# Gate and up with a 512-wide product over both halves of the activations, and weight conversions 1024 wide, in a three-block network on one Trainium2 core

## The chip, the cores and the metric

One core of one Trainium2 chip runs the whole program. The metric is the device time of one launch in microseconds (us). Its engines are TensorE (PE; its weight loads are listed as PEld), VectorE (DVE), ScalarE (ACT), GpSimd (POOL) and SyncE (SP), which issues most DMAs.

## What is computed

The reference sends 256 tokens of width 1024 through two layers of a first block (feed forward, a mixer of retention and gated delta rule, attention to a memory, feed forward) and one second block (state space part, attention, feed forward). All is in float32. The part that the change touches is the feed forward, which occurs five times:

```python
def swiglu(u, w_gate, w_up, w_down):
    return (jax.nn.silu(u @ w_gate) * (u @ w_up)) @ w_down
```

Here `u` is [256, 1024], `w_gate` and `w_up` are [1024, 2816] and `w_down` is [2816, 1024].

## The kernel before

**Products in two parts.** TensorE multiplies in the type float32r, which keeps fewer digits than float32. So each operand is split into a high part, rounded to float32r, and a low part, the remainder, and a product is made of three: high by high, high by low, low by high. `mm3` (L169 to L171) issues these three matmuls. Activations are split where they are transposed (`to_xT`): the high part goes into a tile `xh`, the low part into a tile `xl`, each [128, 8, 256], which is 8 slices of 128 channels by 256 tokens.

**Weights.** `unit` (L133 to L150) loads 1024 columns of weights (512 KB) into one of four `raw` buffers by DMAs of SP's queue (L142). ACT rounds them into `hi` (L147) and DVE subtracts to give `lo` (L148), each in two instructions 512 wide, half after half. The `raw` buffer is free again when both have read it, and only then can SP's next load into it start. The unit lands in one of two pools of weight units, which run well ahead of PE.

**One feed forward (`ffn`).** The 2816 hidden channels go by in 11 groups `j` of 256. Groups 0 and 1 are made with tokens on partitions (`by_tokens`), groups 2 to 10 with channels on partitions: `by_channels(i, j)` makes tile i = 0 or 1 of 128 channels. With 9 groups, 2 tiles and 5 feed forwards there are 90 such tiles. One tile takes, for each of 8 slices k and for a = 0 (gate) and 1 (up), three matmuls of 256 columns: 48 matmuls into one PSUM bank, gate in its columns 0 to 255, up in 256 to 511. DVE then multiplies the bank by the tokens' factors (L400), ACT takes the tanh of the gate (L401), DVE makes the rest of silu and the product with up (L402, L403), and the result is split again into `hh` (ACT, L174) and `hl` (DVE, L176). L174 and L176 are lines of the helper `split`, which splits activations too.

**Order of the work.** `DN(t, j)` multiplies token tile t of group j by the down weights: 12 matmuls of 512 columns, of which the first 6 read tile i = 0 and the last 6 tile i = 1 of `hh` and `hl`. In the middle of a feed forward PE does, group after group,

```python
by_channels(0, j); DN(0, j - 1); by_channels(1, j); DN(1, j - 1)
```

so that tile i = 1 of group j has `DN(1, j - 1)`, the next group's tile i = 0, and half of `DN(0, j)` to be ready in. For j = 2 `DN(1, 0)` stands where `DN(0, 1)` would. The down weights of a group are asked for in `DN`, two units each (one for each i). In the two feed forwards named ffn1 a hook puts a part of the mixer's preparation behind each group. At the end come `DN(0, 8)` to `DN(0, 10)`, then `DN(1, 7)` to `DN(1, 10)`.

Each engine's instructions are put into a fixed order when the program is built, by a scheduler that weighs what each waits for; on the chip each engine takes its own list in that order. So where a weight conversion stands ahead of a tanh in ACT's list, the tanh waits for that conversion, and with it for the conversion's DMA. PSUM has 8 banks, 4 of which hold the sums of the down products in most of a feed forward.

Of the kernel before, what the change touches and what calls it, by code (L numbers as in the profile page):

```python
# [11 lines left out]
F32R = mybir.dt.float32r  # L12
# [10 lines left out]
# columns of the constant table  # L23
C_ID, C_TF, C_SUM, C_ONE = 0, 128, 256, 304
# the ones that only the first block reads
C_TB, C_Z0, C_DN, C_DP, C_HALF, C_END = 304, 432, 560, 944, 1328, 1332
# the ones that only the set-up reads
# [41 lines left out]

class Net:  # L70
    def __init__(self, ctx, tc, a):
# [25 lines left out]
        # instructions that the conversions of weights are queued behind  # L97
        self.fence = []

    def first_block(self, ctx):  # L100
        """what only the first block needs"""
# [17 lines left out]
    def more_weights(self):  # L119
        """a second pool of weight units, kept until no_more_weights()"""  # L120
        if self.w2 is None:
            self.w2_stack = ExitStack()
            self.w2 = self.w2_stack.enter_context(self.tc.tile_pool(name="w2", bufs=8, side="right", reuse_waits="tile"))
        return self.w2
# [9 lines left out]
    def unit(self, loads, n=1024, pool=None, into=None):  # L134
# [8 lines left out]
        with ExitStack() as es:  # L143
            for ins in self.fence:
                es.enter_context(self.tc.issue_after(ins))
            for c in (slice(0, n // 2), slice(n // 2, n)):
# [4 lines left out]
    def prime(self):  # L151
        """the first weights of the next stage, before what its activations wait for"""
# [4 lines left out]
    def unit_rows(self, w, k0, nk, c0, nc_, pool=None):  # L157
        """rows k0*128.. (nk tiles of 128) by columns c0..c0+nc_ of w, as [128, nk, nc_]"""
        hi, lo = self.rows_unit(w, k0, nk, c0, nc_, pool)
# [3 lines left out]
    def rows_unit(self, w, k0, nk, c0, nc_, pool=None, into=None):  # L163
        src = w[k0 * P:(k0 + nk) * P, c0:c0 + nc_].rearrange("(k p) c -> p k c", p=P)
        return self.unit([(lambda r: r[:, :nk * nc_].rearrange("p (k c) -> p k c", k=nk), src)], nk * nc_, pool, into)
# [18 lines left out]
    def rsqrt_half(self, vh, w, eng=None):  # L184
        """v ** -0.5 by Newton steps, given vh = v / 2 > 0 as [128, w]; the sign alternates, so it starts negative"""
# [13 lines left out]
    def half_squares(self, srcs, n):  # L199
        """sums of squares along rows over 2 n, one column for each source"""  # L200
# [16 lines left out]
    def bcast(self, pool, src, w, tag, eng=None):  # L217
        """a row of w values from memory, on all partitions"""
# [10 lines left out]
    def normed(self, src, g, r):  # L229
        """src * r * g, [128, 1024]"""  # L230
# [8 lines left out]
    def new_xT(self):  # L239
        return (self.xp.tile([P, 8, 256], F32R, tag="xh", name="xh"),  # L240
                self.xp.tile([P, 8, 256], F32R, tag="xl", name="xl"))

    def to_xT(self, src, xT, t, k0=0, nk=8, scale=1.0):
        """transposes [128 tokens, nk*128] into xT[:, k0.., t*128..], in two parts that add up exactly"""
# [8 lines left out]
    def set_pre(self, t, g, defer):  # L253
        """the normed activations of the next part: elementwise now, transposes when the part asks. With defer
        the tokens' factors 1 / rms are left to that part, as self.factor"""
# [23 lines left out]
    def run_late(self):  # L279
        """the end of the stage before that the second tokens still miss"""  # L280
# [23 lines left out]
    def gate_up(self, wg, wu, j, q, pool=None):  # L304
# [4 lines left out]
        return self.unit(loads, pool=pool)  # L309

    def ffn(self, wg, wu, wd, gpost_src, post, gpre_src, defer, hook=None, final=None):
        nc = self.nc
        with ExitStack() as es:
# [14 lines left out]
            def wpool(kind, j):  # L328
                # the last units but those for gate and up leave the lasting pool to the next stage
# [5 lines left out]
            def load_gu(j):  # L335
                return [[u.rearrange("p (k a f) -> p k a f", k=2, a=2) for u in self.gate_up(wg, wu, j, q, wpool("gu", j))] for q in range(4)]
# [10 lines left out]
            def by_tokens(t, j, between=None):  # L347
                """one token tile's hidden values, tokens on partitions"""
# [26 lines left out]
            def factor_rows():  # L375
                """half of 1 / rms of the tokens, along the columns of all partitions"""
# [7 lines left out]
            def by_channels(i, j):  # L384
                """one channel tile's hidden values, channels on partitions"""
                if j not in gu:
                    gu[j] = load_gu(j)
                b = self.bank()
                bb = b.rearrange("p (a c) -> p a c", a=2)
                xh, xl = xT  # L390
# [1474 lines left out]
```

## Time and profile before

| what | value |
|---|---|
| three timed runs | 1964.11, 1965.86, 1966.60 us (median 1965.86) |
| span of the profiled execution | 1964.9 us |
| granted clock of TensorE, mean | 0.998 of full speed |
| PE, busy | 1931.5 us (98%) |
| PE weight loads, busy | 1738.6 us (88%) |
| DVE, busy | 1400.5 us (71%) |
| ACT, busy | 1060.7 us (54%) |
| POOL, busy | 182.3 us (9%) |

The profiled execution is recorded by its span, from the first to the last instruction of the core; no other time of it is kept. Busy time of PE includes the time in which one matmul overlaps the next, so a PE that is 98% busy need not be at its peak: how far apart matmuls start says more. Times in a timeline count from the span's start.

### The profile page before, as it was taken

What the parts mean: (1) busy time and instruction counts of PE and PEld (TensorE: products, weight loads), DVE (VectorE), ACT (ScalarE), POOL (GpSimd) and SP (SyncE); (2) the same over time, 40 slices, a digit from 0 to 9 for tenths busy, and PEclk for the clock granted to TensorE, in tenths of its full rate; (3) what the DMA queues carried; (4) which work ended last, traced back from release to release, by engine and by line L of the source; (5) the groups of instructions that cost most, each with busy time, mean ns of one, the idle gap of its engine ahead of it and who ended that gap; (6) DMA issues with size and microseconds to landing.
All of it is one profiled execution on the core that took longest, in us unless ns stands there. A gap on an engine that the chain in (4) does not pass through costs nothing.

```text
span 1964.9 us, 34894 instructions
## 1 busy us (share of the span) xinstructions
PE 1931.5 (98%) x12971; PEld 1738.6 (88%) x12971; DVE 1400.5 (71%) x2981; ACT 1060.7 (54%) x2193; POOL 182.3 (9%) x407
## 2 busy tenths in 40 slices
PE   8999999999999999999999999999999999999998
PEld 6999988898899989999788988998999998888997
DVE  6776688575676666667885747766788988767665
ACT  6655566465555555546554645544555655546542
POOL 2000100020200120010100211002101101001000
PEclk9999999999999999999999999999999999999999
DMA  8666434265465557645433735655466647667651
GB/s 281 193 213 213 129 112 141 83 214 161 150 214 183 171 178 227 198 151 151 135 114 118 232 112 183 203 182 171 131 184 186 173 129 206 199 200 221 195 179 50
DMA packets 272889, 337.28 MB, mean 172 GB/s; under 512 B 19740, under 2 KB 223150, under 8 KB 272718
## 3 DMA queue, kind: packets, MB, share of 16 engines
q1 hardware_dynamic: 266980, 326.64, 53.8%
q10 hardware_dynamic: 5690, 8.25, 1.3%
q8 instruction: 102, 1.67, 0.3%
q14 instruction: 69, 0.57, 0.1%
q0 software_dynamic: 48, 0.16, 0.0%
HBM read 333.90 MB, written 1.08 MB: 170 GB/s over the span
## 4 chain that ended last, share of the span: by engine, by line
PE 82%; DVE 6%; DMA 3%; POOL 3%; issue 3%; ACT 2%; SPq 0%; ACTq 0%; DVEq 0%; POOLq 0%
PE bank L169 24%; PE bank L171 24%; PE bank L170 24%; DVE lo L148 3%; DMA raw<-in_ffn_up_dram 1%; PE bank L1145 1%; POOL t L191 1%; POOL vh L212 1%; PE bank L249 1%; POOL y L192 1%; DMA raw<-in_xattn_k_dram 1%; ACT hi L147 1%; PE bank L1002 1%; PE bank L1542 1%; ACT md L1033 1%
## 5 line engine op out<-in xcount | busy, mean ns | idle before, releaser
L148 DVE TENSOR_TENSOR lo<-raw,hi 128x512 fp32r<-128x512 f32 (+1 forms) x1190 | 765.3, 680 | 219.8 <-ACT hi L147 212.8
L147 ACT ACTIVATE hi<-raw 128x512 fp32r<-128x512 f32 (+1 forms) x1190 | 677.1, 615 | 425.9 <-PE bank L170 96.1
L169 PE MATMUL bank<-xh,hi 128*128 128x256 f32 x2080 | 591.1, 284 | 0.0
L171 PE MATMUL bank<-xh,lo 128*128 128x256 f32 x2080 | 586.8, 282 | 1.0 <-DVE lo L148 1.0
L170 PE MATMUL bank<-xl,hi 128*128 128x256 f32 x2080 | 586.0, 282 | 0.0
L169 PEld LDWEIGHTS bank<-xh,hi 128*128 128x128 f32 x2080 | 394.4, 190 | 3.9
L170 PEld LDWEIGHTS bank<-xl,hi 128*128 128x128 f32 x2080 | 394.3, 190 | 3.4
L171 PEld LDWEIGHTS bank<-xh,lo 128*128 128x128 f32 x2080 | 394.7, 190 | 1.4 <-DVE lo L148 1.4
L169 PE MATMUL bank<-hi,xh 128*128 128x512 f32 (+1 forms) x852 | 334.1, 393 | 5.7 <-ACT xh L174 5.4
L170 PE MATMUL bank<-lo,xh 128*128 128x512 f32 (+1 forms) x852 | 325.5, 382 | 4.4 <-DVE lo L148 4.4
L171 PE MATMUL bank<-hi,xl 128*128 128x512 f32 (+1 forms) x852 | 324.8, 382 | 3.2 <-DVE xl L176 3.2
L169 PEld LDWEIGHTS bank<-hi,xh 128*128 128x128 f32 x852 | 160.9, 189 | 35.0 <-ACT xh L174 7.8
L171 PEld LDWEIGHTS bank<-hi,xl 128*128 128x128 f32 x852 | 160.8, 189 | 33.6 <-DVE xl L176 7.0
L170 PEld LDWEIGHTS bank<-lo,xh 128*128 128x128 f32 x852 | 161.2, 189 | 32.1 <-DVE lo L148 7.3
L169 PE MATMUL bank<-hi,hh 128*128 128x512 f32 x440 | 175.6, 399 | 0.8 <-ACT hh L174 0.8
L171 PE MATMUL bank<-hi,hl 128*128 128x512 f32 x440 | 174.0, 395 | 0.0
L170 PE MATMUL bank<-lo,hh 128*128 128x512 f32 x440 | 173.8, 395 | 0.0
L212 POOL TENSOR_SCALAR vh<-ss 128x1 f32<-128x1 f32 x40 | 27.8, 695 | 1152.3 <-ACT junk L204 1016.0
L401 ACT ACTIVATE th<-s 128x256 f32<-128x256 f32 x90 | 37.3, 415 | 124.1 <-DVE s L400 122.6
L171 PEld LDWEIGHTS bank<-hi,hl 128*128 128x128 f32 x440 | 82.8, 188 | 20.2 <-DVE hl L176 0.2
L169 PEld LDWEIGHTS bank<-hi,hh 128*128 128x128 f32 x440 | 82.7, 188 | 17.4 <-ACT hh L174 1.3
L170 PEld LDWEIGHTS bank<-lo,hh 128*128 128x128 f32 x440 | 82.8, 188 | 16.4
(364 smaller groups left out, 2020.4 us busy)
## 6 DMA issues: line engine op xcount, KB each, us to landing
raw<-in_w_in_dram SPq DMA_DIRECT2D x112, 512.0 KB, 4.2
raw<-in_ffn_gate_dram SPq DMA_DIRECT2D x176, 256.0 KB, 3.9
raw<-in_ffn_up_dram SPq DMA_DIRECT2D x176, 256.0 KB, 4.3
raw<-in_ffn_down_dram SPq DMA_DIRECT2D x88, 512.0 KB, 4.5
raw<-in_w_in_dram SPq DMA_DIRECT2D x96, 192.0 KB, 2.8
raw<-in_w_ffn_gate_dram SPq DMA_DIRECT2D x44, 256.0 KB, 3.8
raw<-in_w_ffn_up_dram SPq DMA_DIRECT2D x44, 256.0 KB, 4.3
raw<-in_w_ffn_down_dram SPq DMA_DIRECT2D x22, 512.0 KB, 4.4
```

Source lines behind the costliest of these rows:

```text
L147: nc.scalar.activation(hi[:, c], raw[:, c], AF.Copy)
L148: nc.vector.tensor_tensor(lo[:, c], raw[:, c], hi[:, c].bitcast(F32), ALU.subtract)
L169: mm(out, lhsT=lh, rhs=rh, start=start, stop=False)
L170: mm(out, lhsT=lh, rhs=rl, start=False, stop=False)
L171: mm(out, lhsT=ll, rhs=rh, start=False, stop=stop)
L191: V.tensor_scalar(t, y, y, vh, ALU.mult, ALU.mult)
L192: V.tensor_scalar(y, t, -1.5, y, ALU.add, ALU.mult)
L212: V.tensor_scalar(vh, s[:, 0:1], s[:, 1:2], 0.5 * EPS, ALU.add, ALU.add)
L249: self.nc.tensor.transpose(b[:, i * P:(i + 1) * P], src[:, (q + i) * P:(q + i + 1) * P], self.ident)
L401: last["A"] = nc.scalar.activation(th, s[:, 0], AF.Tanh)
L1002: T.matmul(b[:, j * 256:(j + 1) * 256], lhsT=lhs[:, h, j * P:(j + 1) * P], rhs=rhs[:, h], start=True, stop=True)
L1033: A.activation(md[r, :, :, :, s], mn[r, :, :, c0:c0 + 16].rearrange("p n h a -> p a h n"), AF.Copy, scale=self.half[s][r])
```

## The change

It has two parts. First, the activations' two parts lie in one tile `xT` of [128, 2, 8, 256], behind a small class `Parts`, so that one matmul can stream the high and the low part of a slice, 512 columns, past the high weights. The products of the high and the low part then lie side by side in a bank, so that gate and up need a bank each. The low weights' matmul, 256 columns, adds to the first half. Afterwards ACT copies the second half to SBUF and DVE adds the first to it, once for gate and once for up; the multiplication by the factors then reads SBUF. Second, weights for gate and up from group 3 on, and down weights from group 2 on, are converted 1024 wide: one ACT and one DVE instruction for each unit in place of two each. The rest of the diff takes out comments.

```diff
+class Parts:
+    def __init__(self, tile_):
+        self.tile = tile_
+    def __getitem__(self, i):
+        if i > 1:
+            raise IndexError
+        return self.tile[:, i]
+    def both(self, k):
+        return self.tile[:, :, k]
...
-            for c in (slice(0, n // 2), slice(n // 2, n)):
+            for c in (slice(0, n),) if whole else (slice(0, n // 2), slice(n // 2, n)):
                 nc.scalar.activation(hi[:, c], raw[:, c], AF.Copy)
                 nc.vector.tensor_tensor(lo[:, c], raw[:, c], hi[:, c].bitcast(F32), ALU.subtract)
...
     def new_xT(self):
-        return (self.xp.tile([P, 8, 256], F32R, tag="xh", name="xh"),
-                self.xp.tile([P, 8, 256], F32R, tag="xl", name="xl"))
+        return Parts(self.xp.tile([P, 2, 8, 256], F32R, tag="xT", name="xT"))
...
-                return [[u.rearrange("p (k a f) -> p k a f", k=2, a=2) for u in self.gate_up(wg, wu, j, q, wpool("gu", j))] for q in range(4)]
+                return [[u.rearrange("p (k a f) -> p k a f", k=2, a=2) for u in self.gate_up(wg, wu, j, q, wpool("gu", j), j > 2)] for q in range(4)]
...
-                b = self.bank()
-                bb = b.rearrange("p (a c) -> p a c", a=2)
-                xh, xl = xT
+                mm = nc.tensor.matmul
+                b = [self.bank() for _ in range(2)]
                 c = slice(i * P, (i + 1) * P)
                 for k in range(8):
                     wh, wl = gu[j][k // 2]
                     for a in range(2):
-                        self.mm3(bb[:, a], wh[:, k % 2, a, c], wl[:, k % 2, a, c], xh[:, k], xl[:, k], k == 0 and a == 0, k == 7 and a == 1)
+                        mm(b[a].rearrange("p (a c) -> p a c", a=2), lhsT=wh[:, k % 2, a, c], rhs=xT.both(k), start=k == 0, stop=False)
+                        mm(b[a][:, 0:256], lhsT=wl[:, k % 2, a, c], rhs=xT[0][:, k], start=False, stop=k == 7)
...
-                nc.vector.tensor_tensor(s, bb, rows[0], ALU.mult)
+                for a in range(2):
+                    nc.scalar.copy(s[:, a], b[a][:, 256:512])
+                    nc.vector.tensor_tensor(s[:, a], b[a][:, 0:256], s[:, a], ALU.add)
+                nc.vector.tensor_tensor(s, s, rows[0], ALU.mult)
...
-                    dn[j] = [self.unit_rows(wd, 2 * j + q, 1, 0, D, wpool("dn", j)) for q in range(2)]
+                    dn[j] = [self.unit_rows(wd, 2 * j + q, 1, 0, D, wpool("dn", j), j > 1) for q in range(2)]
```

In the changed kernel the conversions are L161 and L162, the 512-wide matmul L408, the 256-wide one L409, the copy L415, the addition L416, the multiplication L417, the tanh L418, the two that follow L419 and L420, and the split L188 and L190.

The change alters what each engine's list holds and in which order. **PE**, at the start of tile i = 1 of group 2 in the fourth feed forward (ffn2 of the second layer). The names are the bank, the activations and the weights. Before:

```order
6627 L169 MATMUL bank_13862<-xh_13417,hi_13744 128x256
6628 L170 MATMUL bank_13862<-xl_13418,hi_13744 128x256
6629 L171 MATMUL bank_13862<-xh_13417,lo_13745 128x256
6630 L169 MATMUL bank_13862<-xh_13417,hi_13744 128x256
6631 L170 MATMUL bank_13862<-xl_13418,hi_13744 128x256
6632 L171 MATMUL bank_13862<-xh_13417,lo_13745 128x256
```

Of the change:

```order
5747 L408 MATMUL bank_12943<-xT_12510,hi_12836 128x512
5748 L409 MATMUL bank_12943<-xT_12510,lo_12837 128x256
5749 L408 MATMUL bank_12944<-xT_12510,hi_12836 128x512
5750 L409 MATMUL bank_12944<-xT_12510,lo_12837 128x256
5751 L408 MATMUL bank_12943<-xT_12510,hi_12836 128x512
5752 L409 MATMUL bank_12943<-xT_12510,lo_12837 128x256
```

Six matmuls of 256 columns into one bank became four, two of them of 512 columns, into two banks. The columns are the same in sum, and the order of PE's other work is kept.

**ACT**, around the tanh of the same tile. L147 (now L161) with a `hi` is a conversion of weights; the last two units ahead of `hh` in the second list, like the two on either side of the first list's `hh`, are down weights of group 3. Before:

```order
957 L147 ACTIVATE hi_13959<-raw_13958 128x512 x2
958 L147 ACTIVATE hi_14035<-raw_14034 128x512 x2
959 L147 ACTIVATE hi_14124<-raw_14123 128x512 x2
960 L147 ACTIVATE hi_14142<-raw_14141 128x512 x2
961 L401 ACTIVATE th_13912<-s_13911 128x256
962 L147 ACTIVATE hi_14151<-raw_14150 128x512 x2
963 L147 ACTIVATE hi_14219<-raw_14218 128x512 x2
964 L174 ACTIVATE hh_13839<-th_13912 128x256
965 L147 ACTIVATE hi_14227<-raw_14226 128x512 x2
```

Of the change:

```order
1050 L161 ACTIVATE hi_13160<-raw_13159 128x1024
1051 L415 COPY s_12977<-bank_12943 128x256
1052 L161 ACTIVATE hi_13174<-raw_13173 128x1024
1053 L415 COPY s_12977<-bank_12944 128x256
1054 L161 ACTIVATE hi_13181<-raw_13180 128x1024
1055 L161 ACTIVATE hi_13236<-raw_13235 128x1024
1056 L161 ACTIVATE hi_13242<-raw_13241 128x1024
1057 L418 ACTIVATE th_12978<-s_12977 128x256
1058 L188 ACTIVATE hh_12920<-th_12978 128x256
```

Before, the tanh stood ahead of both down conversions and `hh` between them; now the tanh and `hh` stand behind both.

**DVE**, at the same place. Before:

```order
1490 L400 TENSOR_TENSOR s_13911<-bank_13862,rows_13833 128x512
1491 L148 TENSOR_TENSOR lo_14143<-raw_14141,hi_14142 128x512 x2
1492 L402 SCALAR_TENSOR_TENSOR th_13912<-th_13912,s_13911 128x256
1493 L148 TENSOR_TENSOR lo_14152<-raw_14150,hi_14151 128x512
1494 L403 SCALAR_TENSOR_TENSOR th_13912<-th_13912,s_13911 128x256
1495 L148 TENSOR_TENSOR lo_14152<-raw_14150,hi_14151 128x512
1496 L148 TENSOR_TENSOR lo_14220<-raw_14218,hi_14219 128x512
1497 L176 TENSOR_TENSOR hl_13840<-th_13912,hh_13839 128x256
```

Of the change:

```order
1566 L416 TENSOR_TENSOR s_12977<-bank_12943,s_12977 128x256
1567 L162 TENSOR_TENSOR lo_13175<-raw_13173,hi_13174 128x1024
1568 L416 TENSOR_TENSOR s_12977<-bank_12944,s_12977 128x256
1569 L162 TENSOR_TENSOR lo_13182<-raw_13180,hi_13181 128x1024
1570 L417 TENSOR_TENSOR s_12977<-s_12977,rows_12910 128x512
1571 L162 TENSOR_TENSOR lo_13237<-raw_13235,hi_13236 128x1024
1572 L419 SCALAR_TENSOR_TENSOR th_12978<-th_12978,s_12977 128x256
1573 L162 TENSOR_TENSOR lo_13243<-raw_13241,hi_13242 128x1024
1574 L420 SCALAR_TENSOR_TENSOR th_12978<-th_12978,s_12977 128x256
1575 L190 TENSOR_TENSOR hl_12921<-th_12978,hh_12920 128x256
```

`lo_14220`, and in the second list `lo_13237` and `lo_13243`, belong to down units. The second of the two instructions behind the tanh (L403, now L420) stood ahead of both down units; now it stands behind both.

## Rows read from the trace of the kernel before

**Rows 1.** The page's first part: span, and busy time of each engine.

```profile
span 1964.9 us, 34894 instructions
PE 1931.5 (98%) x12971; PEld 1738.6 (88%) x12971; DVE 1400.5 (71%) x2981; ACT 1060.7 (54%) x2193; POOL 182.3 (9%) x407
```

**Rows 2.** The chain that ended last, by engine.

```profile
PE 82%; DVE 6%; DMA 3%; POOL 3%; issue 3%; ACT 2%; SPq 0%; ACTq 0%; DVEq 0%; POOLq 0%
```

**Rows 3.** All waits of PE; engine, line, releaser, us in all, times, longest.

```profile
PE bank L169 <- ACT hh L174: 0.8, 1, 0.8
```

**Rows 4.** Timeline of PE, group 2 of the fourth feed forward; start and duration in us.

```profile
1220.16 0.40 PE L169 MATMUL bank<-hi,hh 128*128 128x512 f32 x1
...
1222.96 0.28 PE L169 MATMUL bank<-xh,hi 128*128 128x256 f32 x1
...
1228.67 0.40 PE L169 MATMUL bank<-hi,hh 128*128 128x512 f32 x1
...
1230.07 0.40 PE L169 MATMUL bank<-hi,hh 128*128 128x512 f32 x1
```

**Rows 5.** Timeline of PE, first and last of 227 matmuls 512 wide (second block).

```profile
1687.73 0.39 PE L170 MATMUL bank<-lo,ah 128*128 128x512 f32 x1
...
1739.62 0.39 PE L171 MATMUL bank<-hi,yl 128*128 128x512 f32 x1
```

**Rows 6.** Timeline of PE, first and last of 53 matmuls 512 wide (mixer).

```profile
1070.16 0.40 PE L170 MATMUL bank<-lo,xh 128*128 128x512 f32 x1
...
1081.95 0.39 PE L171 MATMUL bank<-hi,xl 128*128 128x512 f32 x1
```

**Rows 7.** Timeline of PE, first and last of 84 down matmuls 512 wide.

```profile
1345.26 0.40 PE L169 MATMUL bank<-hi,hh 128*128 128x512 f32 x1
...
1364.70 0.39 PE L171 MATMUL bank<-hi,hl 128*128 128x512 f32 x1
```

**Rows 8.** Groups by line and shape: count, busy us, mean ns, idle before, releasers.

```profile
L148 DVE TENSOR_TENSOR lo<-raw,hi 128x512 fp32r<-128x512 f32 x1094 | 711.7, 688 | 216.5 <-ACT hi L147 209.6
L147 ACT ACTIVATE hi<-raw 128x512 fp32r<-128x512 f32 x1094 | 629.9, 624 | 384.1 <-PE bank L170 85.7 <-PE bank L171 80.4 <-DMA raw<-in_ffn_up_dram 68.6
L402 DVE SCALAR_TENSOR_TENSOR th<-th,s 128x256 f32<-128x256 f32 x90 | 38.1, 424 | 24.4 <-ACT th L401 24.3
L401 ACT ACTIVATE th<-s 128x256 f32<-128x256 f32 x90 | 37.3, 415 | 124.1 <-DVE s L400 122.6
L176 DVE TENSOR_TENSOR hl<-bank,hh 128x256 fp32r<-128x256 f32 x20 | 8.3, 415 | 0.0
L822 ACT ACTIVATE xg<-ch 128x1024 f32<-128x1024 f32 x4 | 4.4, 1106 | 0.0
L381 ACT COPY rows<-bank 128x256 f32<-128x256 f32 x5 | 1.9, 374 | 3.9 <-PE bank L379 3.8
```

**Rows 9.** Timeline of ACT at the place of rows 4; in brackets idle before, releaser.

```profile
1226.20 1.15 ACT L147 ACTIVATE hi<-raw 128x512 fp32r<-128x512 f32 x2 [1.25 <-DMA raw<-in_ffn_down_dram]
1227.26 0.41 ACT L174 ACTIVATE hh<-th 128x256 fp32r<-128x256 f32 x1
1227.57 1.15 ACT L147 ACTIVATE hi<-raw 128x512 fp32r<-128x512 f32 x2
```

**Rows 10.** Timeline of ACT at the same place of the second, third and fifth feed forwards.

```profile
549.59 1.15 ACT L147 ACTIVATE hi<-raw 128x512 fp32r<-128x512 f32 x2 [0.71 <-DMA raw<-in_ffn_down_dram]
...
742.51 3.24 ACT L147 ACTIVATE hi<-raw 128x512 fp32r<-128x512 f32 x6 [2.17 <-DMA raw<-in_ffn_down_dram]
...
1817.91 1.14 ACT L147 ACTIVATE hi<-raw 128x512 fp32r<-128x512 f32 x2
```

**Rows 11.** Timeline of PE and ACT, group 4 of the fourth feed forward.

```profile
1254.21 0.40 PE L169 MATMUL bank<-hi,hh 128*128 128x512 f32 x1
...
1258.74 0.63 ACT L147 ACTIVATE hi<-raw 128x512 fp32r<-128x512 f32 x1 [1.75 <-DMA raw<-in_ffn_down_dram]
```

**Rows 12.** Timeline of PE, the seventh matmul of a `DN` (first feed forward).

```profile
85.91 0.50 PE L169 MATMUL bank<-hi,hh 128*128 128x512 f32 x1 [0.82 <-ACT hh L174]
```

More of the change, by code (lines that the diff above doesn't have):

```diff
@@ L132, in bank, with unit @@
         return self.ps.tile([P, 512], F32, tag="bank", name="bank")
-    def unit(self, loads, n=1024, pool=None, into=None):
+    def unit(self, loads, n=1024, pool=None, into=None, whole=False):
         if self.stash:
@@ L155, in prime, with unit_rows, rows_unit @@
             self.stash = [u() for u in units]
-    def unit_rows(self, w, k0, nk, c0, nc_, pool=None):
-        hi, lo = self.rows_unit(w, k0, nk, c0, nc_, pool)
+    def unit_rows(self, w, k0, nk, c0, nc_, pool=None, whole=False):
+        hi, lo = self.rows_unit(w, k0, nk, c0, nc_, pool, whole=whole)
         f = lambda w_: w_[:, :nk * nc_].rearrange("p (k c) -> p k c", k=nk)
         return f(hi), f(lo)
-    def rows_unit(self, w, k0, nk, c0, nc_, pool=None, into=None):
+    def rows_unit(self, w, k0, nk, c0, nc_, pool=None, into=None, whole=False):
         src = w[k0 * P:(k0 + nk) * P, c0:c0 + nc_].rearrange("(k p) c -> p k c", p=P)
-        return self.unit([(lambda r: r[:, :nk * nc_].rearrange("p (k c) -> p k c", k=nk), src)], nk * nc_, pool, into)
+        return self.unit([(lambda r: r[:, :nk * nc_].rearrange("p (k c) -> p k c", k=nk), src)], nk * nc_, pool, into, whole)
     def mm3(self, out, lh, ll, rh, rl, start, stop):
@@ L301, in residual, with gate_up @@
             self.set_pre(t, gpre, defer)
-    def gate_up(self, wg, wu, j, q, pool=None):
+    def gate_up(self, wg, wu, j, q, pool=None, whole=False):
         loads = []
@@ L308, in gate_up @@
             loads.append((lambda r, i=i: r.rearrange("p (k a f) -> p k a f", k=2, a=2)[:, :, i, :], src))
-        return self.unit(loads, pool=pool)
+        return self.unit(loads, pool=pool, whole=whole)
     def ffn(self, wg, wu, wd, gpost_src, post, gpre_src, defer, hook=None, final=None):
```

## The prediction

> **What bounds the kernel now.** The page's first part comes first [rows 1]: PE is busy for 98% of a span of 1964.9 us, DVE for 71%, ACT for 54%. The reader sees that there is hardly any idle PE to win back. The chain of waits, which follows the end of the program backwards, says the same: 82% of it is PE [rows 2]. So the time falls if PE's matmuls follow each other more closely, and it rises by every wait put in front of PE. Next, the view of all waits of PE: of the feed forwards' `hh` it lists a single wait, 0.8 us [rows 3]. Everything that the changed tiles hand to the down products is thus in time today, and what counts is with how much room.
>
> The timeline of PE gives the pace. A channel tile runs from 1222.96 to 1228.67, 5.71 us for 48 matmuls, or 118.9 ns from start to start; a `DN` runs from 1220.16 to 1222.96, 2.80 us for 12 [rows 4]. The listed durations (0.28, 0.40 us) overlap and are no price: only the starts are.
>
> **What the merged product saves.** For each slice, and for gate and for up, one 512-wide matmul takes the place of two 256-wide ones, which take 2 x 118.9 = 237.8 ns. There are 90 tiles x 8 x 2 = 1440 such pairs. What is the pace of a 512-wide one? The trace shows it with other operands: 51.89 us over 226 steps, 229.6 ns, in the longest unbroken stretch [rows 5]; 11.79 us over 52, 226.7 ns, in a mixer [rows 6]; 19.44 us over 83, 234.2 ns, in the down products [rows 7]. So a pair saves 8.2 ns by the longest stretch, 11.1 ns by the fastest, 3.6 ns by the slowest: in all 11.8, 16.0 or 5.2 us. I take 11.8, because it is the mean of the most varied operands. The columns are in both cases 768 for a slice of gate or up; only what a matmul costs beyond its columns is saved, which is why the change cannot bring a third of a tile although it takes away a third of its matmuls. No row streams a moving operand in two pieces of 256 columns that lie apart; if that is slower than one piece, the saving shrinks further, and I let the low end go to zero for it.
>
> At this place a rule of the Trainium skill speaks for less. "TensorE: Matmul & The Clock Gate", section "Back-to-back issue gap", gives an isolated matmul N/2.4 + 2.5 ns; two of 256 and one of 512 then differ by 2.5 ns alone, an estimate of 3.6 us for 1440. The trace has 118.9 ns where the rule has 109.2, and 229.6 where it has 215.8, so that its fixed part is too small here; its sum is left as a rival.
>
> **What the evacuation adds.** Each tile gets two copies on ACT and two additions on DVE. The nearest rows: the 256-wide copy out of PSUM, 374 ns, and a 256-wide DVE instruction that reads PSUM, 415 ns [rows 8]. That is 180 x 0.374 = 67 us on ACT and 180 x 0.415 = 75 us on DVE. Against it, the 250 units converted whole (5 x 8 x 4 of gate and up, 5 x 9 x 2 down) go by one instruction instead of two: ACT at 1106 ns [rows 8] instead of 1.15 us for the pair [rows 9], DVE perhaps 1.1 to 1.3 us, where two single ones would be 1.38. So ACT gains about 55 us of work and DVE some 45 to 75, at busy shares of 54% and 71%: neither becomes the bound. Where they are idle this costs nothing. The cover is the time between a tile and its use; what follows is where that cover thins.
>
> **Where the cover thins: `hh` and `hl` of a group's second tile.** Let E be the end of that tile on PE. It is first needed by the seventh matmul of `DN(0, j)`: that it is the seventh, not the first, shows where this wait occurs today [rows 12], since the six before it had started. After E come `DN(1, j - 1)` 2.80, the next tile 5.71 and six matmuls 1.40 [rows 4], so E + 9.91; with a tile shorter by 16 x 8.2 ns = 0.13 us, E + 9.78.
>
> What is ahead of it changes. In the old lists the tanh stands ahead of both down conversions and `hh` between them; in the new lists tanh and `hh` stand behind both on ACT, and L420 behind both on DVE. Each list is taken in order, so the chain now begins when the second down unit has landed, at L: ACT converts it (1.11), tanh (0.415), L419 on DVE (0.424), DVE subtracts the unit (about 1.2), L420 (0.42), `hh` (0.41) [rows 8, 9]. The sum is 3.98, with handovers some 4.1 us: `hh` at L + 4.1.
>
> - Group 2 of the fourth feed forward: E is 1220.16 [rows 4] and the second down unit is converted without a wait at 1227.57 [rows 9], so L is at most about 1227.5, E + 7.3. `hh` comes at E + 11.4 against a need at E + 9.78: a stall of 1.6 us.
> - The same place elsewhere: the second feed forward's conversions of this kind start, after a wait on the DMA, at 549.59, the third's at 742.51 [rows 10], which by the same tile times is as late; I put the first with them. In the fifth, the conversion at 1817.91 does not wait [rows 10] and the landing was about 1.7 us earlier against its tile, so nothing is lost. Four times 1.6 is 6.4 us.
> - Later groups: in group 4, E is 1254.21 and the last down unit's conversion begins at 1258.74 after a wait of 1.75 us on its DMA [rows 11], so L = E + 4.5, `hh` at E + 8.6, over a microsecond early. No stall there, about 25 places.
>
> A stall of this size cannot exceed the whole lateness at one place; if L slips by another microsecond, through raw buffers that come free later, five places cost 2.6 each, 13 us. If the scheduler's lists hide it, zero. I keep 0 to 13.
>
> **Banks.** A tile now takes two banks of the four that the down sums leave. They are free when the copy (0.374) and both additions (0.415 each) are done, about 1.3 us after the tile with handovers, while a `DN` of 2.80 lies between: hidden. Without that cover it costs up to 1.3 us: at the hooks, whose transposes take a bank each, I count two places, 1.5 us, bounds 0 to 3.
>
> **Sum.** -11.8 + 6.4 + 1.5 = -3.9 us, so 1964.9 becomes 1961.0 by the profiled span. The runs' median is 1965.86, 1 us above that span, and the predicted time is against it: 1962.0.
>
> **Rivals.**
> 1. *The stalls do not come.* The saving stands alone, -11.8 (from -5.2 to -16.0): 1954. For it: today's waits are nearly none [rows 3], PE's own pace sets when weights are used, and the stalls rest on one landing time. Against it: ACT's list.
> 2. *The tanh behind the down conversions stalls every group (slower).* If the down units land later than E + 5.7 in the later groups too, by 1.2 us against rows 11, then L + 4.1 passes E + 9.78 in some 25 more places. With landings at E + 6.2 that is 0.5 us each, 12.5 us; together with 13 at group 2 and 1.5 of banks, less 11.8, it is +15: 1981; with half as much in the later groups, +9: 1974.8. For it: the raw buffers come free a half unit later with whole conversions. Against it: a stalled PE gives the loads time, so that the lateness feeds back on itself.
> 3. *The 512-wide product is hardly faster than two 256-wide ones.* At the down products' pace the saving is 5.2, with stalls of 7.9 the sum is +2.7: 1968.5; at no saving, +7.9, 1973.8. That is also how the change would not do what it says. For it: the down products, twelve at a time beside the same tiles, are at that pace [rows 7]. Against it: every other stretch is faster [rows 5, 6]. The page's 2.5 ns above would give +4.3, 1970.2.
>
> **Numbers.** Forecast 0.45, rival 1 0.20, rival 2 0.18, rival 3 0.17. The forecast's own range, 1957 to 1967, has both signs about it. A measurement of this kernel can tell about 0.2% (3.9 us) from no change, so faster means below 1961.9, slower above 1969.8. Faster: half of the forecast and nearly all of rival 1, 0.42. Slower: most of rival 2, over half of rival 3 and a little of the forecast, 0.28. Within: 0.30. The range runs from 1952 (rival 1 without its fastest pace) to 1975 (rival 2 with half as much in the later groups, all of rival 3).
>
> **What would show it.** Right: matmuls L408 and L409 that start 229 and 119 ns apart in a steady tile, some 5.58 us a tile; in PE's waits a new line for `hh` and `hl`, four or five times, 1 to 2 us each, all in group 2; tanh rows that begin just behind a down conversion. Wrong: a 512-wide product near 235 ns or above (rival 3); no wait on `hh` (rival 1); such waits in every group (rival 2); a wait on banks, where PE's first L408 of a tile is released by L416, larger than 3 us in all.

## The result and the profile after

The changed kernel takes 1.0125 times as long as the kernel before, with a 95% interval of 1.0114 to 1.0137: a median of 1991.45 us (1985.03 to 1993.51, 4 runs) against 1965.16. By that ratio it is some 25 us slower, where 4 us less were forecast, and it lies outside the range of 1952 to 1975. Its profiled execution has a span of 1991.6 us; compare [rows 1].

The first lines of the page, the row of the core, and the chain that ended last:

```profile
span 1991.6 us, 31944 instructions
PE 1935.9 (97%) x11531; PEld 1674.5 (84%) x11531; DVE 1452.1 (73%) x2911; ACT 1089.6 (55%) x2123; POOL 181.3 (9%) x407
```

```profile
core 0: 1991.6 us, clock 0.992
```

```profile
PE 69%; DMA 9%; DVE 8%; issue 6%; ACT 4%; POOL 4%; SPq 0%; ACTq 0%; DVEq 0%; POOLq 0%
```

PE's share of the chain fell from 82% [rows 2] to 69%, and DMA's rose from 3% to 9%: PE now stands behind loads. PE has 1440 matmuls fewer and yet is busy for longer, and the mean granted clock is 0.992 where it was 0.998. The view of PE's waits (engine, line, releaser; us, times, longest) names them:

```profile
PE bank L183 <- ACT hh L188: 14.5, 6, 4.5
PE bank L408 <- DVE s L416: 8.0, 7, 2.1
```

The first was 0.8 us [rows 3], the second did not exist. Together that is 21.7 us more. Five of the six waits for `hh` lie at group 2, one in each feed forward; all seven waits for banks lie in the first and third feed forward, the two with hooks.

**One stall, followed through.** Group 2 of the fourth feed forward, the place of [rows 4, 9]. PE's timeline (start, duration; in brackets idle before, releaser): the start of the `DN` ahead, its last matmul before the wait, and what followed.

```profile
1242.32 0.40 PE L183 MATMUL bank<-hi,hh 128*128 128x512 f32 x1
...
1251.91 0.40 PE L185 MATMUL bank<-hi,hl 128*128 128x512 f32 x1
1256.21 0.79 PE L183 MATMUL bank<-hi,hh 128*128 128x512 f32 x1 [3.90 <-ACT hh L188]
1256.81 0.63 PE L184 MATMUL bank<-lo,hh 128*128 128x512 f32 x1
1257.23 0.63 PE L185 MATMUL bank<-hi,hl 128*128 128x512 f32 x1
...
1262.14 0.42 PE L408 MATMUL bank<-xT,hi 128*128 128x512 f32 x1
```

So E, the end of the tile, is 1242.32, and the seventh matmul of `DN(0, 2)` waits for `hh` for 3.90 us. SP's, ACT's and DVE's timelines there:

```profile
1244.63 1.48 SPq L156 DMA_DIRECT2D raw<-in_ffn_down_dram  x2
```

```profile
1251.12 1.06 ACT L161 ACTIVATE hi<-raw 128x1024 fp32r<-128x1024 f32 x1 [1.69 <-DMA raw<-in_ffn_down_dram]
1252.42 1.06 ACT L161 ACTIVATE hi<-raw 128x1024 fp32r<-128x1024 f32 x1 [0.24 <-DMA raw<-in_ffn_down_dram]
1253.38 0.40 ACT L418 ACTIVATE th<-s 128x256 f32<-128x256 f32 x1
1255.74 0.42 ACT L188 ACTIVATE hh<-th 128x256 fp32r<-128x256 f32 x1 [1.96 <-DVE th L420]
```

```profile
1250.61 0.68 DVE L417 TENSOR_TENSOR s<-s,rows 128x512 f32<-128x512 f32 x1
...
1253.81 0.43 DVE L419 SCALAR_TENSOR_TENSOR th<-th,s 128x256 f32<-128x256 f32 x1 [0.38 <-ACT th L418]
1254.16 1.22 DVE L162 TENSOR_TENSOR lo<-raw,hi 128x1024 fp32r<-128x1024 f32 x1
1255.29 0.42 DVE L420 SCALAR_TENSOR_TENSOR th<-th,s 128x256 f32<-128x256 f32 x1
```

The tanh waits for nothing of its own (its input was multiplied by 1251.29): it stands behind two conversions of down weights (those of group 3) that wait for their DMAs. The second began at 1252.42, and `hh` ended at 1256.16, 3.7 us later.

**The stall is paid twice.** The windows of the same stretch (us, PE, PEld, DVE, ACT, POOL, granted clock, DMA share, GB/s):

```profile
1252.00:1255.20 3.20, 0.31 (x2) 0.00 (x0) 2.61 (x3) 1.54 (x3) 0.00 (x0) 1.00 0.75 236
1255.20:1256.20 1.00, 0.00 (x0) 0.00 (x0) 0.52 (x3) 0.46 (x2) 0.00 (x0) 0.59 1.00 340
1256.20:1262.20 6.00, 5.99 (x17) 4.92 (x18) 3.05 (x7) 2.00 (x5) 0.00 (x0) 0.50 0.32 99
1262.20:1264.00 1.80, 1.80 (x12) 1.59 (x12) 1.23 (x1) 1.09 (x2) 0.00 (x0) 1.00 0.00 0
```

PE idles, the granted clock falls from 1.00 to 0.50 (from 2.4 to 1.2 GHz), and when the work resumes it runs at that level until 1262.2. In the PE rows above the 512-wide matmuls then start 0.42 us apart. From 1256.21 to 1262.14 PE did 6 down matmuls and 5 pairs, which take 6 x 0.234 + 5 x 0.351 = 3.16 us in an undisturbed stretch: 2.8 us more are lost, on top of the 3.9 of waiting. There are six such stretches, in five windows of the trace. Each follows one of the six longest of these waits, four for `hh` (2.3 to 4.5 us) and two for banks (2.1 us each):

```profile
60.00:100.00 40.00, 35.55 (x169) 29.32 (x169) 28.29 (x63) 25.14 (x42) 0.00 (x0) 0.91 0.59 187
540.00:600.00 60.00, 57.27 (x295) 48.47 (x294) 42.51 (x62) 31.23 (x49) 0.00 (x0) 0.97 0.65 210
740.00:790.00 50.00, 45.38 (x221) 37.62 (x220) 35.01 (x54) 26.11 (x43) 0.00 (x0) 0.93 0.56 174
860.00:890.00 30.00, 27.86 (x145) 23.75 (x145) 23.80 (x44) 17.51 (x37) 2.31 (x8) 0.94 0.64 200
1240.00:1290.00 50.00, 46.10 (x228) 38.78 (x227) 36.34 (x50) 27.10 (x40) 0.00 (x0) 0.93 0.60 193
```

(1 - 0.91) x 40 + 0.03 x 60 + 0.07 x 50 + 0.06 x 30 + 0.07 x 50 = 14 us, of which a part falls into the waiting itself. Taken in windows of 1 us, and only for the share in which PE was busy, it is some 13; the kernel before has 1.7 of this kind (its rows stand further below), so that 11 are new. **What the merging saves** is in an undisturbed tile, from its first matmul to the next `DN`:

```profile
1302.46 0.39 PE L408 MATMUL bank<-xT,hi 128*128 128x512 f32 x1
...
1308.08 0.39 PE L183 MATMUL bank<-hi,hh 128*128 128x512 f32 x1
```

5.62 us, where it was 5.71 [rows 4]; over 90 tiles some 9 us. So 21.7 of waits and about 11 of lower clock, less 9, is 24, beside 1991.6 - 1964.9 = 26.7 between the two spans; some 3 us are not accounted for.

### The profile page after: what moved, and what is told of

Same layout as the page of the kernel before. It is cut to its first block, busy times and chain, and to the rows that moved or that the text cites. A ratio compares the mean times of both kernels' runs of the same rounds, so it can differ in the third digit from the quotient of the medians.

```text
span 1991.6 us, 31944 instructions
## 1 busy us (share of the span) xinstructions
PE 1935.9 (97%) x11531; PEld 1674.5 (84%) x11531; DVE 1452.1 (73%) x2911; ACT 1089.6 (55%) x2123; POOL 181.3 (9%) x407
## 4 chain that ended last, share of the span: by engine, by line
PE 69%; DMA 9%; DVE 8%; issue 6%; ACT 4%; POOL 4%; SPq 0%; ACTq 0%; DVEq 0%; POOLq 0%
PE bank L183 14%; PE bank L185 14%; PE bank L184 14%; PE bank L408 12%; PE bank L409 6%; DVE lo L162 5%; DMA raw<-in_ffn_up_dram 3%; DMA raw<-in_ffn_down_dram 3%; ACT hi L161 2%; PE bank L1162 1%; POOL t L205 1%; POOL vh L226 1%; POOL y L206 1%; DMA raw<-in_w_ffn_down_dram 1%; PE bank L262 1%
## 5 line engine op out<-in xcount | busy, mean ns | idle before, releaser
L162 DVE TENSOR_TENSOR lo<-raw,hi 128x512 fp32r<-128x512 f32 (+2 forms) x940 | 746.6, 823 | 230.4 <-ACT hi L161 228.6
L161 ACT ACTIVATE hi<-raw 128x512 fp32r<-128x512 f32 (+2 forms) x940 | 652.0, 729 | 410.1 <-PE bank L185 88.4
L408 PE MATMUL bank<-xT,hi 128*128 128x512 f32 x1440 | 516.9, 399 | 8.0 <-DVE s L416 8.0
L409 PE MATMUL bank<-xT,lo 128*128 128x256 f32 x1440 | 408.5, 284 | 0.0
L183 PE MATMUL bank<-hi,xT 128*128 128x512 f32 (+1 forms) x852 | 333.7, 392 | 4.6 <-ACT xT L188 4.5
L408 PEld LDWEIGHTS bank<-xT,hi 128*128 128x128 f32 x1440 | 274.8, 191 | 74.6 <-DVE s L416 10.3
L184 PE MATMUL bank<-lo,xT 128*128 128x512 f32 (+1 forms) x852 | 325.0, 382 | 4.2 <-DVE lo L162 4.2
L185 PE MATMUL bank<-hi,xT 128*128 128x512 f32 (+1 forms) x852 | 324.6, 381 | 3.2 <-DVE xT L190 3.2
L409 PEld LDWEIGHTS bank<-xT,lo 128*128 128x128 f32 x1440 | 275.5, 191 | 3.1
L183 PE MATMUL bank<-hi,hh 128*128 128x512 f32 x440 | 177.3, 403 | 14.5 <-ACT hh L188 14.5
L183 PEld LDWEIGHTS bank<-hi,xT 128*128 128x128 f32 x852 | 160.9, 189 | 33.5 <-ACT xT L188 7.0
L185 PEld LDWEIGHTS bank<-hi,xT 128*128 128x128 f32 x852 | 160.6, 189 | 33.6 <-DVE xT L190 7.1
L183 PE MATMUL bank<-xT,hi 128*128 128x256 f32 x640 | 184.1, 288 | 0.0
L185 PE MATMUL bank<-xT,lo 128*128 128x256 f32 x640 | 180.9, 283 | 1.3 <-DVE lo L162 1.3
L184 PE MATMUL bank<-xT,hi 128*128 128x256 f32 x640 | 180.7, 282 | 0.0
L185 PEld LDWEIGHTS bank<-xT,lo 128*128 128x128 f32 x640 | 121.9, 190 | 1.7 <-DVE lo L162 1.7
L183 PEld LDWEIGHTS bank<-xT,hi 128*128 128x128 f32 x640 | 121.9, 190 | 0.8
L184 PEld LDWEIGHTS bank<-xT,hi 128*128 128x128 f32 x640 | 122.0, 191 | 0.5
```

The source lines that it names most:

```text
L161: nc.scalar.activation(hi[:, c], raw[:, c], AF.Copy)
L162: nc.vector.tensor_tensor(lo[:, c], raw[:, c], hi[:, c].bitcast(F32), ALU.subtract)
L183: mm(out, lhsT=lh, rhs=rh, start=start, stop=False)
L184: mm(out, lhsT=lh, rhs=rl, start=False, stop=False)
L185: mm(out, lhsT=ll, rhs=rh, start=False, stop=stop)
L408: mm(b[a].rearrange("p (a c) -> p a c", a=2), lhsT=wh[:, k % 2, a, c], rhs=xT.both(k), start=k == 0, stop=False)
```

## The experiments

Three theories stood against each other. **A, order:** the new lists put the tanh and `hh` behind the down conversions and their DMAs; the stalls and the lower clock behind them are the loss. **B, conversions:** a whole conversion takes longer from landing to a free raw buffer, so the weights themselves are late. **C, product:** the merged product or its evacuation is what costs. All of these runs have their own runs of the kernel before on the same chip.

**s1, the down conversions moved back behind the hidden tile.**

```diff
+            done_h = {}
...
                 self.split(hh[:, i], hl[:, i], th)
+                done_h[i, j] = self.last
...
                 if j not in dn:
+                    self.fence = done_h.get((1, j - 1), [])
                     dn[j] = [self.unit_rows(wd, 2 * j + q, 1, 0, D, wpool("dn", j), j > 1) for q in range(2)]
+                    if j > 1:
+                        self.fence = []
```

> Edit: the conversions of a group's down weights are queued behind the split of the hidden tile two tiles earlier, so that on ACT the tanh and hh stand ahead of both down conversions again, and on DVE the two instructions behind the tanh and hl too; all else as in the change. Theory A (order: the tanh waits for the down units' DMA, and each such stall is followed by a stretch at the lower clock): PE's waits for hh fall from 14.5 us to under 3 us, the granted clock rises from 0.992 to 0.996 or more, the waits for banks (8.0 us) stay within some 3 us, and the time falls by 14 to 24 us, to 1968 to 1977. Theory B (the whole conversions make the weights themselves late, whatever stands where): PE waits for weights (hi, lo) instead, and the time stays above 1985. Theory C (the merged product or the two banks cost the time): within 5 us of 1991.

Measured: 1.0014 times before (1.0005 to 1.0024), median 1968.06. With the whole conversions and the merged product still in place, 22 of the 25 us are back. PE's waits of this run, and its ACT at the place of the stall (E is 1224.82 here):

```profile
PE bank L409 <- DVE s L417: 4.9, 4, 2.7
...
PE bank L384 <- DVE h L379: 2.5, 3, 1.2
...
PE bank L183 <- ACT hh L188: 1.1, 2, 0.7
```

```profile
1233.18 0.42 ACT L188 ACTIVATE hh<-th 128x256 fp32r<-128x256 f32 x1 [0.95 <-DVE th L421]
1233.50 1.99 ACT L161 ACTIVATE hi<-raw 128x1024 fp32r<-128x1024 f32 x2
```

`hh` now stands ahead of the two conversions and is ready at E + 8.8; its waits fell from 14.5 to 1.1 us. There are no new waits for weights: theory B is out as the main cause, and C too.

The edit does one thing more than its expectation says. The kernel sets a fence of its own ahead of `DN(0, 0)`, which queues conversions behind the first token tile, and lifts it behind `DN(0, 1)`. For groups 0 and 1 `done_h` has no entry, so the edit lifts that fence at once: at the start of the fourth feed forward three down units (of groups 0 and 1) and one unit of gate and up now stand ahead of the first token tile's tanh in ACT's list, where they stood behind it. The line for `h`, a token tile's hidden values, is new among PE's waits, and the loads run earlier from there on (more under "What stays open"). So s1 shows that the lists are the cause, but not how much of the 22 us is the order around the hidden tile alone.

**s2, conversions in halves, all else as in the change.**

```diff
-            for c in (slice(0, n),) if whole else (slice(0, n // 2), slice(n // 2, n)):
+            for c in (slice(0, n // 2), slice(n // 2, n)):
```

> Edit: every conversion in two halves of 512 again; the merged product, two banks, copies and additions stay. Theory A (order): the lists then have one down unit or half of one more behind the tanh, so the waits for hh get shorter, from 14.5 us to some 5 to 10, and the time lies between 1972 and 1985. Theory B (the latency of a whole conversion, about 0.35 us longer from landing to a free raw buffer, passed on by each lap of the four raw buffers): the down units of group 2 land about 1.5 us earlier against their tile than in the change, waits for hh under 5 us, time under 1975. Theory C (merged product and evacuation): within 5 us of 1991.

Measured: 0.9994 (0.9985 to 1.0004), median 1966.00; waits for `hh` 1.3 us. It came out better than A had it, and within B's number. But its lists are other lists. At the place of the stall one of the four down halves stands ahead of the tanh on ACT and the other three between the tanh and `hh`; on DVE, L420 stands ahead of the last three. Here are E (the first row, 1221.68), SP and ACT there:

```profile
1221.68 0.40 PE L183 MATMUL bank<-hi,hh 128*128 128x512 f32 x1
```

```profile
1224.64 0.93 SPq L156 DMA_DIRECT2D raw<-in_ffn_down_dram  x2
```

```profile
1230.13 1.67 ACT L161 ACTIVATE hi<-raw 128x512 fp32r<-128x512 f32 x3
1231.71 0.40 ACT L188 ACTIVATE hh<-th 128x256 fp32r<-128x256 f32 x1
```

The down DMAs did not go out earlier, as B had it: 3.0 us after E, in the change 2.3. Still the second down unit had landed sooner, since its first half, second of the three in the ACT row, began at about E + 9.0 without a wait (in the change E + 10.1). `hh` was ready at E + 10.4, against E + 13.8. So at least 1.1 us of these 3.4 are the landing's, and at most 2.3 the place in the list.

**s3, the product taken apart, the evacuation kept.**

```diff
-  mm(b[a].rearrange("p (a c) -> p a c", a=2), lhsT=wh[:, k % 2, a, c], rhs=xT.both(k), start=k == 0, stop=False)
+  mm(b[a][:, 0:256], lhsT=wh[:, k % 2, a, c], rhs=xT[0][:, k], start=k == 0, stop=False)
+  mm(b[a][:, 256:512], lhsT=wh[:, k % 2, a, c], rhs=xT[1][:, k], start=False, stop=False)
```

> Edit: the 512-wide matmul is two of 256 again, each into its half of the same bank; two banks, copies, additions, whole conversions and the lists of ACT and DVE in the stretches in question stay as in the change. It measures what the merging alone saves: 1440 times 6 ns, 9 us, by the start times of clean tiles in the change's trace (5.61 against 5.71 us). Theory A (order) and theory B (conversions): the stalls stay, so the time is 5 to 12 us above the change, 1996 to 2003. Theory C (the 512-wide product with its two pieces 2048 elements apart costs the time): it falls by over 10 us, below 1981.

Measured: 1.0139 (1.0117 to 1.0160), median 1995.33. That is just under the forecast of A and B. The stalls stay (15.4 us for `hh`), and by the medians it is 4 us slower than the change; the two intervals overlap, so that the times alone say only that the merging saves no more than some 9 us. The trace says more: an undisturbed tile runs from 1302.98 to 1308.69, 5.71 us, as in the kernel before. So the merging does save some 0.10 us a tile, and it is not what costs.

**s4, high and low part side by side.**

```diff
-        return self.tile[:, i]
+        return self.tile[:, :, i]
...
-        return self.tile[:, :, k]
+        return self.tile[:, k]
...
-        return Parts(self.xp.tile([P, 2, 8, 256], F32R, tag="xT", name="xT"))
+        return Parts(self.xp.tile([P, 8, 2, 256], F32R, tag="xT", name="xT"))
```

> Edit: the activations' tile is laid out with high and low part of a slice side by side, so that the 512-wide matmul streams one unbroken piece; all else as in the change. If two pieces are slower than one: its start-to-start time falls from about 232 ns to 227 to 229 and the time by 4 to 8 us. Theories A and B: the pace has nothing to do with the loss, the pace stays at 231 to 234 ns and the time within 5 us of the change.

Measured: 1.0125 (1.0110 to 1.0140), median 1991.03, as the change. An undisturbed tile takes 5.61 us here too (from 1301.11 to 1306.72): two pieces of 256 columns cost no more than one of 512.

**s5, the whole conversions alone, on the kernel before.** The lines that hand the argument `whole` on to `unit` are left out here.

```diff
-            for c in (slice(0, n // 2), slice(n // 2, n)):
+            for c in (slice(0, n),) if whole else (slice(0, n // 2), slice(n // 2, n)):
...
-                return [[u.rearrange("p (k a f) -> p k a f", k=2, a=2) for u in self.gate_up(wg, wu, j, q, wpool("gu", j))] for q in range(4)]
+                return [[u.rearrange("p (k a f) -> p k a f", k=2, a=2) for u in self.gate_up(wg, wu, j, q, wpool("gu", j), j > 2)] for q in range(4)]
...
-                    dn[j] = [self.unit_rows(wd, 2 * j + q, 1, 0, D, wpool("dn", j)) for q in range(2)]
+                    dn[j] = [self.unit_rows(wd, 2 * j + q, 1, 0, D, wpool("dn", j), j > 1) for q in range(2)]
```

> Edit: the kernel before with the whole conversions alone (gate and up from group 3, down from group 2); products, banks and evacuation as before. In group 2 its list of ACT has hh behind both down conversions, with the tanh ahead of them, and L403 ahead of the second. Theory A (order): a shorter lateness than in the change, waits for hh of 2 to 9 us and a few us of lower clock, time 1969 to 1982. Theory B (whole conversions alone are what costs): waits for hh as in the change, 12 us or more, time 1985 or more. Theory C (harmless without the merged product): within 4 us of before.

Measured: 1.0041 (1.0028 to 1.0054), median 1973.18, its single runs from 1968.71 to 1980.86. By its numbers this is A's middle case, but not by the place. Most of the wait for `hh` in the profiled execution (the fastest), 5.1 us, is one stall in the first feed forward, in a later group than 2:

```profile
89.27 0.80 PE L169 MATMUL bank<-hi,hh 128*128 128x512 f32 x1 [4.94 <-ACT hh L174]
```

There too the tanh stands behind a down conversion that waits for its DMA (1.51 us), and `hh` behind one more conversion and a load of a function table (1.28 us) for the hook. At group 2 of the fourth feed forward, which the expectation named, the wait was 0.2 us.

**s6, s1 and s2 together.** On top of s1's edit:

```diff
-            for c in (slice(0, n),) if whole else (slice(0, n // 2), slice(n // 2, n)):
+            for c in (slice(0, n // 2), slice(n // 2, n)):
```

> Edit: the change with conversions in halves and the down conversions queued behind the split of the hidden tile two tiles earlier. Theory A: waits for hh go to 0 to 1 us; what stays are the waits for banks in the feed forwards with hooks (5 to 6 us, and their stretch at the lower clock), so 1961 to 1966, at or a little under before. If the fence itself costs (down weights later): PE waits for lo or hi of down units, 1967 or more.

Measured: 0.9996 (0.9987 to 1.0005), median 1965.68. No waits for `hh` are left among its larger ones, but waits for banks are (4.1 us), and PE waits for `h` of a token tile (2.2 us), as in s1, whose edit this run contains. The edits do not add up: what each takes away is the same stall.

**s7, halves, and the merged product only in the three feed forwards without hooks.** In the first and third, `by_channels` is the one of before.

```diff
+                if hook is None:
                     b = [self.bank() for _ in range(2)]
                     ...
+                else:
+                    b = self.bank()
+                    bb = b.rearrange("p (a c) -> p a c", a=2)
+                    ...
+                            self.mm3(bb[:, a], wh[:, k % 2, a, c], wl[:, k % 2, a, c], xT[0][:, k], xT[1][:, k], k == 0 and a == 0, k == 7 and a == 1)
```

> Edit: conversions in halves; the merged product with its two banks only in the three feed forwards without hooks (second, fourth, fifth), the old tiles in the first and third. If the waits for banks come from the hooks (their transposes, and ACT instructions that wait for the hook's DMAs ahead of the copies): no waits for banks, and the saving of 54 tiles x 0.10 us = 5.4 us less some 1 us of waits for hh shows: 1960 to 1963. If the banks are short in every merged tile: no gain over the kernel with halves everywhere, 1965 to 1967.

Measured: 0.9973 (0.9961 to 0.9984), median 1960.77: **faster than both kernels**, by 5.3 us against before, where 54 tiles at 0.09 to 0.10 us give 4.9 to 5.4. There are no waits for banks left among PE's, the wait for `hh` is 1.2 us, and the stretches above are at full clock:

```profile
PE bank L183 <- ACT hh L188: 1.2, 1, 1.2
```

```profile
60.00:100.00 40.00, 38.80 (x276) 35.80 (x275) 29.54 (x74) 24.70 (x49) 0.00 (x0) 1.00 0.69 212
...
740.00:790.00 50.00, 50.00 (x351) 46.34 (x350) 35.53 (x66) 29.48 (x61) 1.70 (x6) 1.00 0.74 234
```

So the banks are short only in the feed forwards with hooks. In the change, ACT and PE in the first of them show how (same columns as above):

```profile
75.33 0.65 ACT L415 COPY s<-bank 128x256 f32<-128x256 f32 x2 [3.81 <-DMA cwr<-in_gdn_conv_dram]
...
79.12 1.28 ACT L418 ACT_TABLE_LOAD   x1
80.42 0.42 ACT L418 ACTIVATE th<-s 128x256 f32<-128x256 f32 x1
80.74 1.99 ACT L161 ACTIVATE hi<-raw 128x1024 fp32r<-128x1024 f32 x2
82.64 0.40 ACT L188 ACTIVATE hh<-th 128x256 fp32r<-128x256 f32 x1
82.94 0.62 ACT L415 COPY s<-bank 128x256 f32<-128x256 f32 x2
```

```profile
84.06 0.50 PE L408 MATMUL bank<-xT,hi 128*128 128x512 f32 x1 [2.13 <-DVE s L416]
```

The copies that free the banks stand on ACT behind a 3.81 us wait for one of the hook's small loads, and later behind a load of the function table (1.28 us), two whole conversions (1.99 us) and `hh`, one after the other without a gap; PE waits for the addition that follows them. Before, DVE alone emptied a bank (L400).

**s8, s7 with the down conversions moved back as in s1.** On top of s7's edit:

```diff
+                    self.fence = done_h.get((1, j - 1), [])
```

> Edit: the same with the down conversions queued behind the split of the hidden tile two tiles earlier. Theory A: the last waits for hh go, 1 us more: 1959 to 1962. If the fence delays down weights in the hooked feed forwards: 1963 to 1968.

Measured: 0.9985 (0.9976 to 0.9993), median 1962.94: faster than before, but not better than s7, and between its two forecasts. The waits for `hh` fall to 0.7 us; in exchange tiles by tokens wait (2.3 us for `h`, a wait that s7 does not have among its larger ones). This run too lifts the kernel's own fence at the start of each feed forward (see s1), where these token tiles are made; what the new fence does without that was not run.

**s9 and s10, one kind of whole conversion at a time:** gate and up alone, then down alone. The first pair of lines is s9's edit of the change, the second s10's.

```diff
-                    dn[j] = [self.unit_rows(wd, 2 * j + q, 1, 0, D, wpool("dn", j), j > 1) for q in range(2)]
+                    dn[j] = [self.unit_rows(wd, 2 * j + q, 1, 0, D, wpool("dn", j)) for q in range(2)]
...
-                return [[u.rearrange("p (k a f) -> p k a f", k=2, a=2) for u in self.gate_up(wg, wu, j, q, wpool("gu", j), j > 2)] for q in range(4)]
+                return [[u.rearrange("p (k a f) -> p k a f", k=2, a=2) for u in self.gate_up(wg, wu, j, q, wpool("gu", j))] for q in range(4)]
```

> Edit: the change with whole conversions for gate and up alone; down units in halves. Its lists of ACT have the tanh and hh behind all four halves of a group's two down units, as the change has them behind both whole ones; on DVE both instructions behind the tanh stand ahead of the last half. Theory A (order): the stall at group 2 stays, about half a conversion (0.5 us) shorter each: waits for hh of 8 to 14 us, time 1980 to 1991. If whole down conversions are what costs: waits for hh under 4 us, below 1972.

Measured: 1.0094 (1.0079 to 1.0109), median 1985.12, waits for `hh` 10.6 us and for banks 7.0.

> Edit: the change with whole conversions for the down units alone; gate and up in halves. Its lists of ACT have in group 2 one down unit ahead of the tanh and the other between tanh and hh, in later groups both ahead of the tanh. Theory A (order): hh waits for the same last down unit but DVE is done with its instructions behind the tanh earlier; waits for hh of 2 to 9 us, time 1970 to 1982. If whole down conversions are what costs: as the change, 1987 or more.

Measured: 1.0055 (1.0033 to 1.0077), median 1973.98; waits for `hh` among the larger ones are two of 1.6 and 0.9 us, for `hl` 2.7 in all, for banks 6.5. Both fall where theory A had them: s9, where all of the down conversions stand ahead of the tanh although they are in halves, waits twice as long as s10 (10.6 us against 5.2 for `hh` and `hl` together), where in group 2 one of the two units stands behind it. So the width of the down conversions does not set the loss: halves ahead of the tanh cost more than whole ones of which one stands behind it.

## Why the prediction was wrong

- **Bound and pace: right.** PE's starts were the thing to price, and a wait in front of PE the danger. The first step that was off is a size: the merged pair saves some 0.09 to 0.10 us a tile, 9 us in all, not 11.8. With a low product at its old 119 ns, the 512-wide one starts after 232 ns, between the longest stretch and the down products [rows 5, 7]. The doubt whether two pieces might be slower than one was needless (s4).
- **Evacuation: right in price, wrong in place.** The copy took 368 ns and the addition 418, against 374 and 415 [rows 8]. But "I count two places, 1.5 us" for the banks was 8.0 us in seven places, over the bound of 3 and the sign of being wrong that the prediction had set there: I asked only whether a `DN` lies in between, not what stands ahead of the copy on ACT.
- **The chain behind the tanh: right mechanism, right chain, wrong landing.** I gave the chain 4.1 us from the landing to `hh`, and it took 3.7 from the conversion's start. The step that failed is the landing, "L is at most about 1227.5, E + 7.3": taken from the trace before [rows 9], it was E + 10.1 after. 2.0 us of this come from the down DMAs, which went out at E + 2.3 instead of E + 0.3 (the row below, of the kernel before, where E is 1220.16); the rest is that they took longer, 7.8 us to the second conversion's start against at most 7.0. A landing time is itself an outcome of the lists, and I carried it over unchanged.

```profile
1220.48 1.54 SPq L142 DMA_DIRECT2D raw<-in_ffn_down_dram  x2
```

The stalls came out at 14.5 us instead of 6.4, nearly all where forecast, in group 2: 2.3, 2.7, 4.5, 3.9 and 0.9 us in the five feed forwards, where 1.6 in each of four and none in the fifth were forecast. The upper bound of 13, for a landing one microsecond later, was about reached.
- **No price for the clock: the term that was missing.** Each of the six longest waits for `hh` and banks was followed by work at 1.2 GHz, some 13 us in all, 11 more than before. The trace before shows the price, at a place that I did not look at, outside the feed forwards, in the attention to the memory: a wait of 1.32 us, and behind it 4 us at a mean of 0.57 of full speed, 1.7 us lost (columns of the window as above).

```profile
1142.66 0.50 PE L169 MATMUL bank<-hi,xh 128*128 128x512 f32 x1 [1.32 <-ACT xh L174]
```

```profile
1144.00:1148.00 4.00, 4.00 (x12) 3.15 (x11) 0.95 (x4) 1.02 (x4) 0.00 (x0) 0.57 0.10 33
```

The sum with the measured saving and waits but without the clock is -9 + 13.7 + 8.0 = +13, 1979 us, already over the range; with the clock's 11 it is 1990, beside 1991.45 measured.
- **The rivals.** Rival 2 (slower, by the tanh behind the conversions) had the cause and the sign; it looked for its size in the later groups, where there is a single wait for `hh`, of 0.2 us, and not in what a stall costs afterwards. Rival 3, the pace, was wrong: it costs 3 us of the forecast and no more. The isolated gap of the Trainium skill's page "TensorE: Matmul & The Clock Gate", section "Back-to-back issue gap", gave 3.6 us of saving; the trace shows 9.

**What stays open:** why the down DMAs at this place went out 2 us later against their tile than in the kernel before, and so how much of a stall is the list's and how much the loads'. In s1 they went out 0.3 us ahead of E:

```profile
1224.50 1.48 SPq L156 DMA_DIRECT2D raw<-in_ffn_down_dram  x2
...
1224.82 0.40 PE L183 MATMUL bank<-hi,hh 128*128 128x512 f32 x1
```

ACT's lists of s1 and of the change are the same from the start of group 2 to this tanh, but not at the start of the feed forward (see s1), and s1 was ahead well before: its pair of down DMAs before this one went out 17.4 us ahead of E, that of the change 14.4 us. First s1's row, then that of the change:

```profile
1207.44 1.48 SPq L156 DMA_DIRECT2D raw<-in_ffn_down_dram  x2
```

```profile
1227.93 1.48 SPq L156 DMA_DIRECT2D raw<-in_ffn_down_dram  x2
```

With the change's list and s1's loads, `hh` would come at E - 0.3 + 7.8 + 3.7 = E + 11.2, an estimate from the change's 7.8 us between DMA and second conversion and its chain of 3.7. PE asks for it at E + 9.8, and in s1 it was ready at E + 8.8. So by this estimate the list makes a stall even with early loads, of 1.4 us, and late loads make it longer. A run with a fifth raw buffer would tell whether the buffers set the loads' time; it was not made.

## What to carry to other kernels

Before costing an edit in a kernel whose lists are made by a scheduler, look at what stands between an engine's short instructions that PE waits for and the loads that fill its list: a conversion ahead of a tanh ties PE to a DMA. Price a wait of PE at what it idles plus the work that then runs at the lower clock; here 3.9 us became 6.7. And where a change buys a little pace for another engine in the path that frees PSUM, use it only where that engine's list is quiet: in three of five places it was worth 5 us, in all five at best nothing (s2 and s6).

## What was not expected of the hardware

The clock. In the stall above its level fell to half while PE was idle, between 1255.2 and 1256.2, and did not rise when the work resumed at 1256.21 but at 1262.2, after PE had been busy all the while. A wait of 3.9 us thus cost 6.7. And a 512-wide product whose moving operand lies in two pieces 8 KB apart was exactly as fast as one in one piece (5.61 us a tile).
